# A two-layer encoder on one core: token halves grouped over six tail and eight head k-tiles, and a ring of nine split weight pairs

## The chip, the core and the metric

One core of a Trainium2 chip. The time is the device time of one execution in microseconds (us). The profile is of one execution.

## What is computed

A two-layer encoder for 256 tokens of width 2048, in fp32. Cut to what matters here:

```python
for l in range(2):
    h = rms_norm(x, norm_g[l, 0])
    m = parallel_ab_mixer(h, ...) if l == 0 else chunk_band_attention(h, ...)   # ends in "@ w_out"
    x = x + rms_norm(m, norm_g[l, 1])
    f = (silu(h2 @ w_gate[l]) * (h2 @ w_up[l])) @ w_down[l]   # h2 = rms_norm(x, norm_g[l, 2])
    x = x + rms_norm(f, norm_g[l, 3])
```

rms_norm divides a token's row by its root mean square, so no token of a block's output is finished before that token's whole row of the last product is there.

## The kernel before

The 256 tokens are two halves of 128, t = 0 and 1. Every product is cut into column chunks of 512 and k-tiles of 128 rows. Each weight is read once: SP's queue brings two k-tiles as one `raw` tile of 512 KB (L224, four buffers). ACT casts each k-tile to the fp32r tile `hi` (L230), DVE subtracts to get `lo` (L231). Five such pairs (`wpool`, bufs=5) can be alive. For each k-tile and token half, `mm_chunk` issues three 128x512 matmuls, hi with the activation's hi (L250), lo with its hi (L251), hi with its lo (L252). The two halves alternate k-tile by k-tile, each in its own PSUM tile `mm_...`.

The stages are, in order, w_in with layer 0's mixer, w_oab (4 chunks of 16 k-tiles), w_gu0 (22 chunks of 16), w_dn0 (4 of 44), w_qkv with the attention, w_oc (4 of 16), w_gu1 and w_dn1. w_oab, w_dn0, w_oc and w_dn1 end in `out_norm`, the next stage begins with `pre_norm`.

`out_norm` squares each chunk's rows on ACT (L317) and scales them on DVE. In the last of its four chunks, n = 3, the last four k-tiles have their pairs in a pool E of their own and run all for half 0, then all for half 1. When a half is done: ACT Square (L317) and sqrt (L319), DVE L320 (PSUM times the gain row, into `m`), reciprocal (L321), then four residual operations (L323), one for each column slice of 512; these make the next block's input `m_o_0` to `m_o_3` (`m_fo_...` after an FFN). The very last out_norm sends each piece to HBM.

`pre_norm` takes the four slices one by one. PE transposes 128x128 blocks (L286) into PSUM tiles `pn_...`, each with two k-tiles of both halves. ACT (L268) writes the hi part of a k-tile `sh`, DVE (L269) the lo part `sl`, each 128x256. The norm's scale is applied after the product, so the next stage's first matmuls wait for `sh` and `sl` alone.

The engines run their queues in order. The order is set by the Tile scheduler from priorities: the weight stream is PRI_STREAM (4000) ahead of its place in the program, the norms are PRI_NORM (8000) ahead; waits between engines are semaphores that the framework sets from tile uses.

Of the kernel before, what the change touches and what calls it, by code (L numbers as in the profile page):

```python
# [24 lines left out]
PRI_NORM = 8000  # L25
PRI_FIRST = 100000
# [113 lines left out]
def encoder_body(ctx: ExitStack, tc: tile.TileContext, A):  # L140
# [5 lines left out]
    wpool = ctx.enter_context(tc.tile_pool(name="wpool", bufs=5))  # L146
    S = ctx.enter_context(tc.tile_pool(name="S", bufs=12))
# [116 lines left out]
    def split_evac(ps, sh, sl, kts, g):  # L264
        """ps [P, 2, T] (feature-major) times the feature column g(kt), split into hi and lo."""
        for i, kt in enumerate(kts):
            gc = g(kt)
            last = act.activation(sh[:, kt % 4, :], ps[:, i, :], AF.Copy, scale=gc)  # L268
            dve.scalar_tensor_tensor(sl[:, kt % 4, :], ps[:, i, :], gc, sh[:, kt % 4, :].bitcast(F32),  # L269
                                     op0=ALU.mult, op1=ALU.subtract)  # L270
        return last

    def pre_norm(xt, gname, tag):
        """xt: 4 token-major tiles [P, 2, 512]. Returns split x*g, feature-major, and its row scale."""
        st = []
        evacs.clear()
        for n in range(4):
            sh = S.tile([P, 4, T], F32R, tag="S", name=f"sh_{tag}_{n}")
            sl = S.tile([P, 4, T], F32R, tag="S", name=f"sl_{tag}_{n}")
# [9 lines left out]
            st.append((sh, sl))  # L289
# [10 lines left out]
    def out_norm(ctx2, wname, st, grow, xres, tag, last=False):  # L300
        """x + rms_norm(st @ w) * g; returns 4 token-major tiles."""
        E = ctx2.enter_context(tc.tile_pool(name="E" + tag, bufs=4, reuse_waits="tile"))
# [4 lines left out]
        for n in range(4):  # L307
# [3 lines left out]
            ps = mm_chunk(wname, n, st, tail=E if n == 3 else None)  # L311
# [26 lines left out]
    def ffn(l, xt):  # L338
        st, rs = pre_norm(xt, f"g{l}2", f"f{l}")
        with ExitStack() as mx:  # L340
            hp = mx.enter_context(tc.tile_pool(name=f"ff{l}", bufs=2 * NFF, reuse_waits="tile"))
            hid = []
            for j in range(NFF):
                pg = mm_chunk(f"w_gu{l}", 2 * j, st)
# [19 lines left out]
            return out_norm(mx, f"w_dn{l}", hid, 2 * l + 1, xt, f"fo{l}", last=l == 1)  # L364

# [1 line left out]
    def mixer0(xt):  # L367
# [3 lines left out]
        with ExitStack() as mx:  # L371
# [11 lines left out]
            def proj(n, width=512):  # L383
                """Token-major rows of the in-projection, scaled: [P, 2, 512]."""
# [6 lines left out]
            def tr2(tm, c0s, width=P, name=""):  # L391
                """Two feature tiles, transposed: PSUM [P, 2, T]."""
# [6 lines left out]
            def shift_mix(ps, out, mi, n=P):  # L399
                """out = p + (shift(p) - p) * mu, feature-major [n, T]; mi: column of mu."""  # L400
# [18 lines left out]
            # dt = softplus(p + bias): max(x, 0) + 2 atanh(e / (2 + e)), e = exp(-|x|)  # L419
# [33 lines left out]
            def rwkv_half(hf):  # L453
# [7 lines left out]
                for which in range(3):  # L461
# [20 lines left out]
                    if which == 0:  # L482
                        # decay logs, in-chunk running sums, in-context rates, unit keys
# [56 lines left out]
                        # in-chunk products, masked: rows b|k, columns a|r  # L540
# [11 lines left out]
                        # (I - N)^-1 of the 32-blocks, block (chunk, head) on a partition  # L552
# [15 lines left out]
                # bonus: sum(r k r_k) v  # L568
# [6 lines left out]
                # token-major b|k and v  # L575
# [12 lines left out]
                # S = (I - N)^-1 of the 64-blocks, from the 32-blocks  # L588
# [20 lines left out]
                # chunks in order  # L609
# [61 lines left out]
                # group norm per token and head  # L671
# [42 lines left out]
            def conv_silu(ps, i, ft, out):  # L714
                """Causal 4-tap convolution and SiLU of one feature tile: out [P, T]."""
# [23 lines left out]
            # exp of running sums: to the end of tile 0, from the start of tile 1  # L739
# [66 lines left out]
            for g in range(2):  # L806
# [29 lines left out]
    def mixer1(xt):  # L836
# [3 lines left out]
        with ExitStack() as mx:  # L840
# [3 lines left out]
            for g in range(4):  # L844
# [3 lines left out]
                for which in range(2):  # L848
                    ps2 = mm_chunk("w_qkv", 3 * g + which, st)
# [55 lines left out]
            return out_norm(mx, "w_oc", ost, 2, xt, "o1")  # L905
# [21 lines left out]
```

## Time and profile before

| what | value |
| --- | --- |
| median of 3 runs | 2416.78 us (2416.41 to 2418.41) |
| profiled execution | span 2412.1 us, first to last instruction, 4.7 us less than the median of the runs |
| PE matmul busy | 2372.9 us, 98% |
| DVE, ACT busy | 59%, 53% |
| chain that ended last | PE 94%, DVE 4%, ACT 1% |
| DMA | 178 GB/s mean, 429 MB |
| mean granted TensorE clock | 0.992 |

The time is set by PE. A busy share says little about the places where PE stops; these are found in the list of PE's waits and in the timelines around them. The granted clock is given as a share of full speed: 1.00 is 2.4 GHz and 0.50 is 1.2 GHz.

### The profile page before, as it was taken

To read this page: it belongs to the slowest core of one execution; us is meant where nothing else is said; L and a number is where in the kernel's file an instruction comes from. 1 tells how busy PE (TensorE), PEld (TensorE's weight loads), DVE (VectorE), ACT (ScalarE), POOL (GpSimd) and SP (SyncE) were. 2 spreads that over 40 slices of the span, in tenths; PEclk is the share of its full clock that TensorE was granted. 3 is DMA by queue.
4 is the path that set the end of the run, shared out by engine and by line. 5 is a ranking of instruction groups with operands and counts; after the bars stand their busy time and mean duration, and the time that the engine had idled before them with its cause. 6 is when DMAs were issued, how large, how long until landed. Compare 5 with 4: busy or idle time off the path is not lost.

```text
span 2412.1 us, 31517 instructions
## 1 busy us (share of the span) xinstructions
PE 2372.9 (98%) x11374; PEld 1940.9 (80%) x11374; DVE 1424.3 (59%) x2340; ACT 1267.4 (53%) x2232; POOL 33.2 (1%) x60
## 2 busy tenths in 40 slices
PE   8999999999999999999999999999999999999998
PEld 7777778878888888888877888887888888888887
DVE  5865967665555555555556555556555555555554
ACT  6646545656445445444446555555544544544443
POOL 0000000000000000000000000000000000000000
PEclk9999999999999999999999999999999999999999
DMA  7433424656666666666675555565666666666665
GB/s 229 142 113 112 140 88 132 190 181 189 192 185 191 192 185 191 192 187 196 196 229 153 180 178 160 172 191 172 189 189 189 190 189 191 189 188 193 199 197 158
DMA packets 119358, 429.17 MB, mean 178 GB/s; under 512 B 13409, under 2 KB 13665, under 8 KB 119201
## 3 DMA queue, kind: packets, MB, share of 16 engines
q1 hardware_dynamic: 115424, 415.46, 56.6%
q0 software_dynamic: 2400, 9.18, 1.5%
q10 hardware_dynamic: 1376, 2.52, 0.3%
q8 instruction: 89, 1.46, 0.3%
q14 instruction: 69, 0.56, 0.1%
HBM read 425.01 MB, written 2.10 MB: 177 GB/s over the span
## 4 chain that ended last, share of the span: by engine, by line
PE 94%; DVE 4%; ACT 1%; issue 1%; DMA 1%; SPq 0%; POOL 0%; DVEq 0%; ACTq 0%; POOLq 0%
PE mm_w_gu L250 13%; PE mm_w_gu L252 13%; PE mm_w_gu L251 13%; PE mm_w_dn L251 7%; PE mm_w_dn L252 7%; PE mm_w_dn L250 7%; PE mm_w_qkv L250 4%; PE mm_w_qkv L251 4%; PE mm_w_qkv L252 4%; PE mm_w_in L252 3%; PE mm_w_in L251 3%; PE mm_w_in L250 3%; PE mm_w_oc L252 1%; PE mm_w_oc L251 1%; PE mm_w_oab L251 1%; PE mm_w_oab L252 1%
## 5 line engine op out<-in xcount | busy, mean ns | idle before, releaser
L231 DVE TENSOR_TENSOR lo_w_gu<-raw_w_gu,hi_w_gu 128x512 fp32r<-128x512 f32 x704 | 486.7, 692 | 433.3 <-ACT hi_w_gu L230 432.4
L230 ACT CAST hi_w_gu<-raw_w_gu 128x512 fp32r<-128x512 f32 x704 | 438.3, 623 | 473.4 <-DVE lo_w_gu L231 424.9
L250 PE MATMUL mm_w_gu<-hi_w_gu,sh_f 128*128 128x512 f32 x1408 | 551.3, 392 | 0.7 <-ACT sh_f L268 0.7
L251 PE MATMUL mm_w_gu<-lo_w_gu,sh_f 128*128 128x512 f32 x1408 | 551.3, 392 | 0.0
L252 PE MATMUL mm_w_gu<-hi_w_gu,sl_f 128*128 128x512 f32 x1408 | 549.2, 390 | 0.0
L231 DVE TENSOR_TENSOR lo_w_dn<-raw_w_dn,hi_w_dn 128x512 fp32r<-128x512 f32 x352 | 242.4, 692 | 218.5 <-ACT hi_w_dn L230 218.2
L230 ACT CAST hi_w_dn<-raw_w_dn 128x512 fp32r<-128x512 f32 x352 | 217.2, 621 | 246.5 <-DVE lo_w_dn L231 233.1
L250 PEld LDWEIGHTS mm_w_gu<-hi_w_gu,sh_f 128*128 128x128 f32 x1408 | 265.1, 188 | 55.6 <-ACT sh_f L268 1.2
L252 PEld LDWEIGHTS mm_w_gu<-hi_w_gu,sl_f 128*128 128x128 f32 x1408 | 265.0, 188 | 54.2
L251 PEld LDWEIGHTS mm_w_gu<-lo_w_gu,sh_f 128*128 128x128 f32 x1408 | 265.2, 188 | 53.2
L251 PE MATMUL mm_w_dn<-lo_w_dn,hh 128*128 128x512 f32 x704 | 276.8, 393 | 0.0
L252 PE MATMUL mm_w_dn<-hi_w_dn,hl 128*128 128x512 f32 x704 | 275.3, 391 | 0.0
L250 PE MATMUL mm_w_dn<-hi_w_dn,hh 128*128 128x512 f32 x704 | 274.8, 390 | 0.0
L231 DVE TENSOR_TENSOR lo_w_qkv<-raw_w_qkv,hi_w_qkv 128x512 fp32r<-128x512 f32 x192 | 132.5, 692 | 102.9 <-ACT hi_w_qkv L230 102.6
L230 ACT CAST hi_w_qkv<-raw_w_qkv 128x512 fp32r<-128x512 f32 x192 | 118.9, 621 | 108.6 <-DVE lo_w_qkv L231 65.5
L231 DVE TENSOR_TENSOR lo_w_in<-raw_w_in,hi_w_in 128x512 fp32r<-128x512 f32 x184 | 125.0, 689 | 56.1 <-ACT hi_w_in L230 54.9
L250 PEld LDWEIGHTS mm_w_dn<-hi_w_dn,hh 128*128 128x128 f32 x704 | 132.1, 188 | 30.1
L250 PE MATMUL mm_w_in<-hi_w_in,sh_in 128*128 128x512 f32 (+1 forms) x384 | 154.5, 402 | 1.4 <-ACT hi_w_in L230 1.4
L252 PE MATMUL mm_w_in<-hi_w_in,sl_in 128*128 128x512 f32 (+1 forms) x384 | 155.2, 404 | 0.0
L251 PEld LDWEIGHTS mm_w_dn<-lo_w_dn,hh 128*128 128x128 f32 x704 | 132.3, 188 | 28.4
L251 PE MATMUL mm_w_qkv<-lo_w_qkv,sh_qkv 128*128 128x512 f32 x384 | 155.1, 404 | 0.0
L252 PEld LDWEIGHTS mm_w_dn<-hi_w_dn,hl 128*128 128x128 f32 x704 | 132.2, 188 | 27.8
(335 smaller groups left out, 2837.5 us busy)
## 6 DMA issues: line engine op xcount, KB each, us to landing
raw_w_gu<-in_w_gu SPq DMA_DIRECT2D x352, 512.0 KB, 3.6
raw_w_dn<-in_w_dn SPq DMA_DIRECT2D x176, 512.0 KB, 4.2
raw_w_qkv<-in_w_qkv SPq DMA_DIRECT2D x96, 512.0 KB, 3.6
raw_w_in<-in_w_in SPq DMA_DIRECT2D x92, 512.0 KB, 3.6
raw_w_oab<-in_w_oab SPq DMA_DIRECT2D x32, 512.0 KB, 3.7
raw_w_oc<-in_w_oc SPq DMA_DIRECT2D x32, 512.0 KB, 4.2
bias<-in_bias POOLq DMA_DIRECT2D x4, 768.0 KB, 7.5
x_in<-in_x SPq DMA_DIRECT2D x4, 512.0 KB, 10.3
```

Source lines behind the costliest of these rows:

```text
L230: act.copy(hi, raw[:, h, :])
L231: dve.tensor_tensor(lo, raw[:, h, :], hi.bitcast(F32), op=ALU.subtract)
L250: pe.matmul(o, lhsT=xh, rhs=h_[:, :width], start=k_ == 0, stop=False)
L251: pe.matmul(o, lhsT=xh, rhs=l_[:, :width], start=False, stop=False)
L252: pe.matmul(o, lhsT=xl, rhs=h_[:, :width], start=False, stop=k_ == nk - 1)
```

## The change

Two numbers are added, HEAD = 8 and TAIL = 6. In the last chunk of every out_norm the last six k-tiles run for half 0, then for half 1. In the first chunk of w_gu0, w_qkv and w_gu1 the first eight k-tiles do so. The pool E is gone. From w_oab on (a second pool `wx` is opened when layer 0's mixer pools are closed) the pairs go round a ring of nine, five in `wpool` and four in `wx`; w_in still has five. For slices 0 and 1 of these three pre_norms a PSUM tile `ph_...` holds four k-tiles of one half, with priority PRI_EVAC (9000); its evacuation pieces are 128x128 (L294 on ACT, L295 on DVE, 16 each where eight 128x256 stood). Slices 2 and 3 stay as they were. Comments are removed, which shifts line numbers: L230, L231, L250 to L252, L317 to L323 become L235, L236, L255 to L257, L334 to L340.

```diff
+PRI_EVAC = 9000
+HEAD, TAIL = 8, 6
...
+    ring = [wpool]
+    turn = [0]
...
-            wp = tail if tail is not None and u >= nk // 2 - 2 else wpool
...
                 for h in range(2):
+                    wp = ring[turn[0] % len(ring)]
+                    turn[0] += 1
...
-        skew = 4 if tail is not None else 0
-        for kt, (hi, lo) in enumerate(stream(wname, n, nk, tail)):
+        for kt, (hi, lo) in enumerate(stream(wname, n, nk)):
             held.append((kt, hi, lo))
-            if kt < nk - skew or kt == nk - 1:
+            if head - 1 <= kt < nk - tail or kt == nk - 1:
...
     def pre_norm(xt, gname, tag):
+        split = 0 if tag == "in" else 2
+        for t in range(2):
+            for n in range(split):
+                sh, sl = st[n]
+                with tc.high_priority(offset=PRI_EVAC):
+                    ps = psa.tile([P, 4, P], F32, tag="sa", name=f"ph_{tag}_{n}_{t}")
+                    for i in range(4):
+                        pe.transpose(ps[:, i, :], xt[n][:, t, i * P:(i + 1) * P], ident)
+                    for i in range(4):
+                        gc = col(gname, 4 * n + i)
+                        xh = sh[:, i, t * P:(t + 1) * P]
+                        last = act.activation(xh, ps[:, i, :], AF.Copy, scale=gc)
+                        dve.scalar_tensor_tensor(sl[:, i, t * P:(t + 1) * P], ps[:, i, :], gc, xh.bitcast(F32),
+                                                 op0=ALU.mult, op1=ALU.subtract)
+        for n in range(split, 4):
...
-        E = ctx2.enter_context(tc.tile_pool(name="E" + tag, bufs=4, reuse_waits="tile"))
...
-            ps = mm_chunk(wname, n, st, tail=E if n == 3 else None)
+            ps = mm_chunk(wname, n, st, tail=TAIL if n == 3 else 0)
...
-                pg = mm_chunk(f"w_gu{l}", 2 * j, st)
+                pg = mm_chunk(f"w_gu{l}", 2 * j, st, head=HEAD if j == 0 else 0)
```

**The first boundary, PE.** `mm_w_oab_0` and `mm_w_oab_1` are the two halves of the last w_oab chunk, `mm_w_gu_0_0` and `mm_w_gu_0_1` those of the first w_gu0 chunk; `hi_w_oab_7_1` is the last k-tile. Before:

```order
L251 MATMUL mm_w_oab_1_4642<-lo_w_oab_7_1_4792,ybh_4033 128x512
L286 MATMUL pn_f_0_0_4842<-cc,m_o_0_4254 128x128 x2
L286 MATMUL pn_f_0_1_4851<-cc,m_o_0_4254 128x128 x2
L252 MATMUL mm_w_oab_1_4642<-hi_w_oab_7_1_4791,ybl_4034 128x512
L286 MATMUL pn_f_0_0_4842<-cc,m_o_0_4254 128x128 x2
L286 MATMUL pn_f_0_1_4851<-cc,m_o_0_4254 128x128 x2
L250 MATMUL mm_w_gu_0_0_4946<-hi_w_gu_0_0_0_4950,sh_f_0_4840 128x512
```

After:

```order
L256 MATMUL mm_w_oab_1_4642<-lo_w_oab_7_0_4776,ybh_4033 128x512
L290 MATMUL ph_f_0_0_4847<-cc,m_o_0_4254 128x128 x4
L290 MATMUL ph_f_1_0_4860<-cc,m_o_1_4443 128x128 x4
L257 MATMUL mm_w_oab_1_4642<-hi_w_oab_7_0_4775,ybl_4034 128x512
L255 MATMUL mm_w_oab_1_4642<-hi_w_oab_7_1_4779,ybh_4033 128x512
L256 MATMUL mm_w_oab_1_4642<-lo_w_oab_7_1_4780,ybh_4033 128x512
L257 MATMUL mm_w_oab_1_4642<-hi_w_oab_7_1_4779,ybl_4034 128x512
L255 MATMUL mm_w_gu_0_0_4961<-hi_w_gu_0_0_0_4965,sh_f_0_4839 128x512
```

Half 0's transposes now stand four matmuls ahead of half 1's end and need two residual tiles; half 1's (`ph_f_0_1`, `ph_f_1_1`) stand in the head, 16 matmuls after its first.

**The first boundary, DVE, from half 0's end.** Before:

```order
L231 TENSOR_TENSOR lo_w_gu_0_2_0_4995<-raw_w_gu_0_2_4992,hi_w_gu_0_2_0_4994 128x512
L320 TENSOR_TENSOR m_o_3_4819<-mm_w_oab_0_4641,gb_o_3_4639 128x512
L321 RECIPROCAL rs_o_4073<-rs_o_4073 128x1
L323 SCALAR_TENSOR_TENSOR m_o_0_4254<-m_o_0_4254,rs_o_4073,x_x_0_4060 128x512
L323 SCALAR_TENSOR_TENSOR m_o_1_4443<-m_o_1_4443,rs_o_4073,x_x_1_4062 128x512
L323 SCALAR_TENSOR_TENSOR m_o_2_4630<-m_o_2_4630,rs_o_4073,x_x_2_4064 128x512
L323 SCALAR_TENSOR_TENSOR m_o_3_4819<-m_o_3_4819,rs_o_4073,x_x_3_4066 128x512
L320 TENSOR_TENSOR m_o_3_4819<-mm_w_oab_1_4642,gb_o_3_4639 128x512
```

After:

```order
L337 TENSOR_TENSOR m_o_3_4819<-mm_w_oab_0_4641,gb_o_3_4639 128x512
L338 RECIPROCAL rs_o_4073<-rs_o_4073 128x1
L236 TENSOR_TENSOR lo_w_gu_0_1_1_4980<-raw_w_gu_0_1_4973,hi_w_gu_0_1_1_4979 128x512
L340 SCALAR_TENSOR_TENSOR m_o_0_4254<-m_o_0_4254,rs_o_4073,x_x_0_4063 128x512
L340 SCALAR_TENSOR_TENSOR m_o_1_4443<-m_o_1_4443,rs_o_4073,x_x_1_4065 128x512
L340 SCALAR_TENSOR_TENSOR m_o_2_4630<-m_o_2_4630,rs_o_4073,x_x_2_4067 128x512
L295 SCALAR_TENSOR_TENSOR sl_f_0_4840<-ph_f_0_0_4847,pf,sh_f_0_4839 128x128
L340 SCALAR_TENSOR_TENSOR m_o_3_4819<-m_o_3_4819,rs_o_4073,x_x_3_4069 128x512
L295 SCALAR_TENSOR_TENSOR sl_f_1_4842<-ph_f_1_0_4860,pf,sh_f_1_4841 128x128
L295 SCALAR_TENSOR_TENSOR sl_f_0_4840<-ph_f_0_0_4847,pf,sh_f_0_4839 128x128
L236 TENSOR_TENSOR lo_w_gu_0_3_0_4996<-raw_w_gu_0_3_4993,hi_w_gu_0_3_0_4995 128x512
```

Ahead of half 0's end five `lo` of the next stage were made before (k-tiles 0 to 4) and three are now; the fourth stands between the reciprocal and the first residual, others among the residuals and pieces. On ACT, likewise, the casts of k-tiles 3 to 8 stand behind half 0's sqrt.

**The end of layer 0's mixer, ACT.** `rs_gr` is the last norm's root there, `ybh` the evacuation of the mixer's output. Before:

```order
L260 ACT_TABLE_LOAD
L260 ACTIVATE rs_gr<-rs_gr 128x2
L230 CAST hi_w_in_7_0_3994<-raw_w_in_7_3992 128x512
L230 CAST hi_w_in_7_1_3998<-raw_w_in_7_3992 128x512
L268 ACTIVATE ybh_3816<-yb_3818,pf 128x256
```

After:

```order
L235 CAST hi_w_oab_0_0_4080<-raw_w_oab_0_4078 128x512
L265 ACT_TABLE_LOAD
L265 ACTIVATE rs_gr<-rs_gr 128x2
L235 CAST hi_w_in_7_0_3994<-raw_w_in_7_3992 128x512
L235 CAST hi_w_in_7_1_3998<-raw_w_in_7_3992 128x512
L235 CAST hi_w_oab_1_0_4102<-raw_w_oab_1_4100 128x512
L235 CAST hi_w_oab_0_1_4084<-raw_w_oab_0_4078 128x512
L235 CAST hi_w_oab_2_0_4124<-raw_w_oab_2_4122 128x512
L235 CAST hi_w_oab_1_1_4106<-raw_w_oab_1_4100 128x512
L273 ACTIVATE ybh_3816<-yb_3818,pf 128x256
```

Five casts of w_oab now stand ahead of the first `ybh`, one of them ahead of the sqrt. POOL's and SP's orders are unchanged.

## Rows read from the trace of the kernel before

**Rows 1.** PE's waits: engine, line, waited for, us in total, times, longest.

```profile
PE pn_f L286 <- DVE m_o L323: 5.0, 2, 2.6
...
PE pn_qkv L286 <- DVE m_fo L323: 2.5, 1, 2.5
```

**Rows 2.** Timeline, first boundary, half 0: start, duration, engine, line, operation [idle before].

```profile
521.55 0.39 PE L252 MATMUL mm_w_oab<-hi_w_oab,ybl 128*128 128x512 f32 x1
...
522.70 0.69 DVE L320 TENSOR_TENSOR m_o<-mm_w_oab,gb_o 128x512 f32<-128x512 f32 x1 [2.11 <-ACT junk_o L317]
...
523.50 2.74 DVE L323 SCALAR_TENSOR_TENSOR m_o<-m_o,rs_o,x_x 128x512 f32<-128x512 f32 x4
```

**Rows 3.** Timeline, first boundary, half 1's end and the next stage's start.

```profile
524.78 0.48 PE L252 MATMUL mm_w_oab<-hi_w_oab,ybl 128*128 128x512 f32 x1
525.30 0.60 ACT L317 ACTIVATE junk_o<-mm_w_oab 128x512 bf16<-128x512 f32 x1 [2.30 <-PE mm_w_oab L252]
...
527.75 0.66 PE L286 MATMUL pn_f<-cc,m_o 128*128 128x128 f32 x4 [2.49 <-DVE m_o L323]
...
528.75 0.80 PE L250 MATMUL mm_w_gu<-hi_w_gu,sh_f 128*128 128x512 f32 x1 [0.35 <-ACT sh_f L268]
```

**Rows 4.** Windows after the three boundaries: length, busy us by engine, PEclk, DMA.

```profile
528.00:533.00 5.00, 4.65 (x18) 3.60 (x17) 3.49 (x8) 2.31 (x5) 0.00 (x0) 0.66 0.23 52
1269.00:1273.00 4.00, 4.00 (x14) 3.16 (x13) 2.87 (x6) 1.47 (x3) 0.00 (x0) 0.57 0.12 31
1668.00:1673.00 5.00, 5.00 (x18) 4.00 (x18) 3.38 (x7) 2.15 (x6) 0.00 (x0) 0.66 0.27 54
```

**Rows 5.** PE's timeline after two stops in layer 0's mixer.

```profile
159.02 1.18 PE L599 MATMUL ga<-TG,AA 32*32 32x32 f32 x31 [2.71 <-DVE TG L594]
...
253.91 0.63 PE L396 MATMUL tr<-cc,tm 128*128 128x128 f32 x4 [2.19 <-DVE r L402]
254.29 0.48 PE L250 MATMUL mm_w_in<-hi_w_in,sh_in 128*128 128x512 f32 x1
254.61 0.40 PE L251 MATMUL mm_w_in<-lo_w_in,sh_in 128*128 128x512 f32 x1
254.84 0.39 PE L252 MATMUL mm_w_in<-hi_w_in,sl_in 128*128 128x512 f32 x1
```

**Rows 6.** Windows after these two stops, columns as in rows 4.

```profile
254.00:255.00 1.00, 1.00 (x7) 0.91 (x8) 1.00 (x3) 0.42 (x2) 0.00 (x0) 1.00 0.84 262
...
160.00:165.00 5.00, 5.00 (x77) 4.29 (x75) 0.00 (x0) 1.17 (x3) 0.00 (x0) 0.50 0.35 108
```

**Rows 7.** Instruction groups by form: count, busy us, mean ns, idle before by releaser.

```profile
L231 DVE TENSOR_TENSOR lo_w_gu<-raw_w_gu,hi_w_gu 128x512 fp32r<-128x512 f32 x704 | 486.7, 692 | 433.3 <-ACT hi_w_gu L230 432.4
L230 ACT CAST hi_w_gu<-raw_w_gu 128x512 fp32r<-128x512 f32 x704 | 438.3, 623 | 473.4 <-DVE lo_w_gu L231 424.9 <-PE mm_w_gu L252 40.3 <-DMA raw_w_gu<-in_w_gu 3.8
...
L269 DVE SCALAR_TENSOR_TENSOR sl_f<-pn_f,pf,sh_f 128x256 fp32r<-128x256 f32 x32 | 14.3, 478 | 1.0 <-ACT sh_f L268 0.9
L268 ACT ACTIVATE sh_f<-pn_f,pf 128x256 fp32r<-128x256 f32 x32 | 13.8, 470 | 6.2 <-PE pn_f L286 5.4 <-DVE sl_f L269 0.8
L323 DVE SCALAR_TENSOR_TENSOR m_fo<-m_fo,rs_fo,m_o 128x512 f32<-128x512 f32 x16 | 11.0, 748 | 0.1
...
L902 ACT CAST oh<-ov 128x256 fp32r<-128x256 f32 x16 | 5.6, 375 | 3.8 <-PE ov L901 3.5
```

**Rows 8.** Timeline of the kernel's end.

```profile
2402.49 2.74 DVE L323 SCALAR_TENSOR_TENSOR m_fo<-m_fo,rs_fo,m_o 128x512 f32<-128x512 f32 x4
...
2403.27 0.39 PE L252 MATMUL mm_w_dn<-hi_w_dn,hl 128*128 128x512 f32 x1
...
2404.42 0.29 ACT L319 ACTIVATE rs_fo<-ssq_fo,part_fo 128x1 f32<-128x1 f32 x1
2405.15 0.68 DVE L320 TENSOR_TENSOR m_fo<-mm_w_dn,gb_fo 128x512 f32<-128x512 f32 x1
2405.75 0.15 DVE L321 RECIPROCAL rs_fo<-rs_fo 128x1 f32<-128x1 f32 x1
```

More of the change, by code (lines that the diff above doesn't have):

```diff
@@ L211, in encoder_body, with stream @@
     dve.tensor_scalar(hcv, pf[:, _PF["conv_w"]:_PF["conv_w"] + 60], 0.5, None, op0=ALU.mult)
-    def stream(wname, n, nk, tail=None):
+    def stream(wname, n, nk):
         src = A[wname]
         for u in range(nk // 2):
-            wp = tail if tail is not None and u >= nk // 2 - 2 else wpool
             with tc.high_priority(offset=PRI_STREAM):
@@ L233, in stream, with mm_chunk @@
             yield from pair
-    def mm_chunk(wname, n, st, width=512, tail=None):
+    def mm_chunk(wname, n, st, width=512, head=0, tail=0):
         nk = 4 * len(st)
@@ L273, in pre_norm @@
     def pre_norm(xt, gname, tag):
-        st = []
+        st = [(S.tile([P, 4, T], F32R, tag="S", name=f"sh_{tag}_{n}"),
+               S.tile([P, 4, T], F32R, tag="S", name=f"sl_{tag}_{n}")) for n in range(4)]
         evacs.clear()
-        for n in range(4):
-            sh = S.tile([P, 4, T], F32R, tag="S", name=f"sh_{tag}_{n}")
-            sl = S.tile([P, 4, T], F32R, tag="S", name=f"sl_{tag}_{n}")
+        split = 0 if tag == "in" else 2
[13 more added lines that the diff above has]
+        for n in range(split, 4):
+            sh, sl = st[n]
             with tc.high_priority(offset=PRI_NORM):
@@ L288, in pre_norm @@
                     evacs.append(last)
-            st.append((sh, sl))
         ssq = sm.tile([P, 2, 4], F32, tag="ssq", name=f"ssq_{tag}")
@@ L298, in pre_norm, with out_norm @@
         return st, rsqrt_mean(ssum, D, EPS, "pre", [P, 2])
-    def out_norm(ctx2, wname, st, grow, xres, tag, last=False):
-        E = ctx2.enter_context(tc.tile_pool(name="E" + tag, bufs=4, reuse_waits="tile"))
+    def out_norm(wname, st, grow, xres, tag, last=False):
         ssq = sm.tile([P, 2, 4], F32, tag="ssq", name=f"ssq_{tag}")
@@ L363, in ffn @@
                 hid.append((sh, sl))
-            return out_norm(mx, f"w_dn{l}", hid, 2 * l + 1, xt, f"fo{l}", last=l == 1)
+            return out_norm(f"w_dn{l}", hid, 2 * l + 1, xt, f"fo{l}", last=l == 1)
     def mixer0(xt):
@@ L830, in mixer0 @@
                 yst.append((sh, sl))
+        wx = ctx.enter_context(tc.tile_pool(name="wx", bufs=4, reuse_waits="tile"))
+        ring[:] = [wpool, wx, wpool, wx, wpool, wx, wpool, wx, wpool]
         with ExitStack() as mx:
             xres = load_x(mx.enter_context(tc.tile_pool(name="X0", bufs=4, reuse_waits="tile")), "x0")
-            return out_norm(mx, "w_oab", yst, 0, xres, "o0")
+            return out_norm("w_oab", yst, 0, xres, "o0")
     def mixer1(xt):
@@ L848, in mixer1 @@
                 for which in range(2):
-                    ps2 = mm_chunk("w_qkv", 3 * g + which, st)
+                    ps2 = mm_chunk("w_qkv", 3 * g + which, st, head=HEAD if g + which == 0 else 0)
                     tm = B.tile([P, 2, 512], F32, tag="tm", name=f"qk{g}{which}")
@@ L904, in mixer1 @@
                 ost.append((sh, sl))
-            return out_norm(mx, "w_oc", ost, 2, xt, "o1")
+            return out_norm("w_oc", ost, 2, xt, "o1")
     x1 = mixer0(x_in)
```

## The prediction

> **What bounds the kernel now.** The table above says that PE is busy for 98% of the span and that the chain which ended last is PE for 94% of its length. Matmuls of 128x512 start 0.23 us apart when nothing stops them [rows 5]. The change adds and removes none of them, so it can move the time only where PE stops, or where it runs at the lower clock. I therefore read PE's waits first. The transposes at the head of a stage wait for the residual tiles `m_o` and `m_fo`: 5.0 us in two waits and 2.5 us in one [rows 1], that is about 2.5 us at each of the three boundaries w_oab to w_gu0, w_dn0 to w_qkv and w_oc to w_gu1.
>
> The timeline of the first boundary shows the chain behind one wait. Half 0 ends with the matmul at 521.55, its scaling L320 starts 1.15 us later, its four residuals 1.95 us later [rows 2]. Half 1 ends 12 matmuls after half 0, with the matmul at 524.78. Its own chain (L317, sqrt, L320, L321, L323) only delivers `m_o_0` of half 1 at 527.75, so PE stands for 2.49 us. After four transposes it stands again, for 0.35 us, until ACT has evacuated the first tile [rows 3]. Last, I read the clock. In the 5, 4 and 5 us after these stops the mean granted clock is 0.66, 0.57 and 0.66 [rows 4], so (1 - 0.66) x 5, (1 - 0.57) x 4 and again 0.34 x 5 = 1.7 us of full-rate work is lost each time.
>
> One boundary thus costs 2.5 + 0.35 of waiting, 1.7 of half clock, and about 0.1 for each of two restarts (the first two matmuls after a stop start 0.32 apart where later ones are 0.23 apart [rows 5]): **4.75 us**, 14.2 us for three.
>
> **The change at a boundary.** With six k-tiles grouped instead of four, half 0 ends two k-tiles, 6 x 0.23 = 1.4 us, earlier and its chain starts 1.4 us earlier. With eight k-tiles grouped in the first chunk, the new order of PE has 16 matmuls (3.7 us) of half 0 ahead of half 1's transposes. That covers half 1's chain of 3.0 us (524.78 to 527.75), so the long stop goes. What is late next is the work that makes the head's operands. I walk it in the clock of [rows 2, 3].
>
> Half 0's last matmul starts at 521.55 - 1.4 = 520.2, L337 at 521.3, the reciprocal ends near 522.1. In the new order of DVE the `lo` of k-tile 3 stands ahead of the first residual. Its cast takes a ring slot that half 1's first tail k-tile gives back, and ACT is with Square and sqrt until about 521.6 (sqrt ends 1.44 us after the half's last matmul has started, as from 2403.27 to 2404.71 [rows 8]). Cast 0.62 and `lo` 0.69 [rows 7] bring DVE to 522.9; with residuals 0.685 apart (2.74 for four [rows 2]) `m_o_0` is there at 523.6 and `m_o_1` at 524.3. PE has then done 14 of its 18 half-1 matmuls (520.4 + 14 x 0.23 = 523.6), transposes `m_o_0` (0.38 [rows 5]) and waits some 0.35 for `m_o_1`. The last four matmuls end at 525.7, and the head begins.
>
> Its evacuation pieces are 128x128, which no row has. From 128x256 and 128x512 of a like kind [rows 7] DVE's is 478 - (748 - 478)/2 = 343 ns and ACT's 470 - (623 - 375)/2 = 346 ns: my estimate is 0.35 each, the other end is the full 0.47. Four pieces lie in one PSUM tile, where ACT and DVE take turns, so a k-tile is ready every 0.35 + 0.35 + two hand-offs = 0.8 us, more when a cast, Square (0.60 [rows 3]) or a residual stands between, while PE eats a k-tile of one half in 0.69. k-tiles 0 and 1 are in time; I count 0.4 for k-tile 2 and 0.55 for k-tile 3, 0.35 for the second pair of transposes (`m_o_0` of half 1 stands behind L337, the reciprocal, a `lo` and three pieces), and 0.75 for the first k-tiles of half 1 and k-tile 4. With the 0.35 above that is **2.4 us** of waiting. About eight stops at 0 to 0.1 for a restart: 0.4. The boundary then costs 2.8 instead of 4.75, **1.95 less, 5.85 for three**, if the clock stays up.
>
> The ends of this term: in the stretch DVE has 8 residuals (5.5), L337 (0.7), 16 pieces (5.5) and some five `lo` (3.5), together 15.2 us, against PE's 66 matmuls (15.2) and 16 transposes (1.5), 16.7 us. DVE fits, but with little room. If all overlaps, only 0.35 and 0.65 of it are left (1.0). If it queues badly, or the pieces cost 0.47 each, 16 x 0.12 = 1.9 more on DVE, of which 1.5 shows (4.2).
>
> Why does this not vanish as the ring grows? Nine pairs hold six tail pairs and three of the head; before, four tail pairs lay in pool E and five of the head were cast in advance. Five casts of the head's eight therefore fall into the boundary where three did.
>
> **The clock.** A stop of 2.19 us before 253.91 was followed by a clock of 1.00, and a stop of 2.71 before 159.02 by 0.50 from 160 to 165 [rows 5, 6]. The walk leaves no stop over 0.6, with full matmuls between them, and the first three of a head together (0.35 + 0.4 + 0.55) are shorter than the one that kept 1.00. I take the 1.7 as won in full.
>
> The Trainium skill, page "TensorE: Matmul & The Clock Gate", section "A second HAM failure mode: psum-queue depth-cycling", speaks against this: it tells of a kernel whose PE idles briefly but often between groups of matmuls and whose clock swings between the two levels. No row of before has such a run of short stops, so it stands as a rival below; by it the 1.7 would be paid again.
>
> **The other parts.** *End of the kernel.* The last out_norm gets the six-tile tail without a head. In before L320 of half 1 starts only at 2405.15, behind half 0's four residuals (2402.49 + 2.74), though sqrt ended at 2404.71 [rows 8]. With half 0 1.4 us earlier the residuals end at 2403.9, L320 by 2404.5, and the reciprocal waits for sqrt: it starts near 2404.75 instead of 2405.75. **1.0 less**; between 0.7 (a hand-off more) and 1.2. *Ring.* From w_oab on four more casts stand ahead of mixer0's last work on ACT: one ahead of the sqrt that the first `yb` transposes wait for (0.62 [rows 7]), twice at most, the rest ahead of evacuations that PE needs only in w_oab's later k-tiles. 0 to 1.2; with what deeper casting displaces in the attention stage (0 to 0.8) I take **+0.8**. *FFN stages.* Casts run up to nine k-tiles ahead; the list behind [rows 1] has no wait of PE for a cast of these stages, and ACT idles as long as it casts [rows 7], so 0. *DMA, POOL and SP* keep their order and `raw` its four buffers: 0.
>
> **Sum.** -5.85 - 1.0 + 0.8 = -6.05 us. The profiled execution has a span of 2412.1, the median of the runs is 4.7 us longer; I take what lies around the span as unchanged, so from 2416.78 the forecast is **2410.7 us**. A measurement can tell about 0.2% (4.8 us, so below 2411.95) from no change.
>
> **The rivals.**
> *B, the clock falls once per head.* For it: eight stops and 16 transposes in some 9 us, nothing like which before shows. Against it: the 2.19 us stop. Price 1.7 x 3 = 5.1, so 2415.8, within 0.2%.
> *D, DVE and ACT become the bound.* For it: 15.2 us of DVE work in 16.7, and the strict turns in a PSUM tile. Against it: ACT's 16 pieces (5.5), two Squares with accumulator and sqrt (2.2) and five casts (3.1) are 10.8 us of the 16.7. Price 4.2 - 2.4 = 1.8 of which some 1.1 shows at each boundary, so +3.3: 2414.0, within 0.2%.
> *C, slower.* The clock drops at the first stops and stays low until the stops end: some 8.5 us of head and then 3.4 as in [rows 4], 12 us at half clock, as it stayed at 0.50 from 160 to 165 and beyond under a stream of small work [rows 6]. It costs 6.0 less the 1.6 of waits that slower matmuls hide, 4.4 x 3 = 13.2: 2423.9. It is slower from 11 us in all, 3.7 per boundary. Against it: the matmuls in the head are full ones.
> *N, nothing gained.* The transposes put among the last half-1 matmuls wait longer than 0.35 and move the old stop ahead: every 0.7 us (one residual more ahead of `m_o_1`) costs 2.1; 2412.8 with one, counted under D.
>
> **How the numbers follow.** The forecast's case gets 0.66; its own spread, waits of 1.6 to 3.4 us per boundary (2.4 less to 3.0 more in three) and the bounds of the small terms, is 2407.5 to 2414, of which 0.52 lies below 2411.95 and 0.14 above. B gets 0.12, D with N 0.15 (0.02 of it below the line), C 0.07. Faster 0.54, same 0.39, slower 0.07. The range reaches up to B with a little over it and down to the forecast's lower end: 2407.0 to 2416.2; C lies outside.
>
> **What will show it.** PE's waits for `m_o` of 2.5 us are gone and 5 to 9 waits of 0.1 to 0.6 each stand at a boundary, on `sh_f`, `sl_f` and `ph_f`, 2.4 us in all (1.0: overlap better than walked; 4: D). The granted clock stays 1.00 in the 15 us after each (0.50 in any: B or C). The last reciprocal starts 1.0 us nearer to the last matmul (2405.75 - 2403.27 = 2.5 now [rows 8], 1.5 then). Wrong would be new PE waits for casts in the FFN stages, or stops where the ring opens above 1.2 us.

## The result: slower, with the long stops gone

The changed kernel takes 2437.11 us (median of 4 runs, 2435.0 to 2438.2), the kernel before on the same chip 2417.28. The ratio is 1.008, 95% interval 1.0065 to 1.0094. I forecast 2410.7, faster, with a range up to 2416.2: wrong in sign and outside the range. One execution of the kernel before (2960.93 us) and one of a variant (13552.62 us) lie far outside all others and are left out of the medians below.

The page of the changed kernel, first its span and engines:

```profile
span 2433.2 us, 31534 instructions
...
PE 2400.9 (99%) x11374; PEld 1937.6 (80%) x11374; DVE 1425.6 (59%) x2364; ACT 1267.9 (52%) x2256; POOL 33.2 (1%) x60
```

The span grew by 21.1 us, and PE's busy time by 28.0 (from 2372.9) for the same 11374 matmuls. So PE does not wait more; its matmuls take longer. The list of PE's waits (us in total, times, longest) confirms the first half. Its only rows on the boundaries and the ring are:

```profile
PE yb L845 <- DVE xs L837: 0.8, 1, 0.8
PE mm_w_gu L255 <- ACT sh_f L294: 0.5, 2, 0.3
...
PE mm_w_qkv L255 <- ACT sh_qkv L294: 0.2, 1, 0.2
```

The waits of 5.0 and 2.5 us for the residual tiles [rows 1] are gone. The windows over the three boundaries (length, busy us of PE, PEld, DVE, ACT, POOL, then granted clock, DMA share, GB/s) show that the half clock of [rows 4] is gone too:

```profile
528.00:543.00 15.00, 14.63 (x69) 9.89 (x68) 14.37 (x34) 9.94 (x28) 0.54 (x1) 1.00 0.39 116
...
1276.00:1286.00 10.00, 9.66 (x44) 6.10 (x42) 9.86 (x24) 6.53 (x20) 0.54 (x1) 1.00 0.29 79
1676.00:1686.00 10.00, 9.65 (x45) 6.25 (x43) 9.91 (x24) 6.58 (x19) 0.54 (x1) 1.00 0.29 79
```

Now a stretch in which PE waits for nothing, 400 us in the middle of w_gu0, instructions on its PSUM tiles alone (length, then PE, PEld, DVE, ACT, clock). The kernel before:

```profile
600.00:1000.00 400.00, 396.03 (x1727) 322.66 (x1726) 12.63 (x18) 12.10 (x18) 1.00 0.63 189
```

The changed kernel:

```profile
600.00:1000.00 400.00, 396.30 (x1697) 316.57 (x1696) 12.63 (x18) 12.35 (x18) 1.00 0.62 186
```

At the same clock, 30 matmuls fewer fit: 231.6 us per thousand before, 235.7 now (the transposes between them included). The length of each stage, from its first to its last matmul start in the two traces, gives the account:

| stage | before | after | change, us |
| --- | --- | --- | --- |
| ahead of w_oab | 436.1 | 439.6 | +3.5 |
| w_oab | 88.6 | 90.8 | +2.2 |
| w_gu0, w_gu1 | 492.8, 492.9 | 501.8, 501.7 | +17.7 |
| w_dn0, w_dn1 | 242.9, 242.4 | 245.6, 244.5 | +4.9 |
| w_qkv with the attention | 303.7 | 307.2 | +3.4 |
| w_oc | 91.0 | 92.5 | +1.5 |
| from one stage to the next, w_oab on | 12.6 | 1.4 | -11.3 |
| last matmul start to the end | 8.78 | 8.08 | -0.7 |

The 29.6 us in the stages from w_oab on are the loss. Some 4 of them come with the new order, the short stops and the transposes that moved into the stages, and stand against the 11 us saved between the stages (in two kernels compared below, which differ by the change but not in the spacing of their matmuls, it is 3.7). The other 26 are spread over all stages. Of the 3.5 us ahead of w_oab 0.7 is a later start and 0.8 the new wait for `xs`; the rest goes with more half clock in layer 0's mixer, where the order is unchanged. One window there, of the changed kernel:

```profile
250.00:262.00 12.00, 9.81 (x50) 6.98 (x49) 10.72 (x20) 5.04 (x10) 1.97 (x4) 0.86 0.55 174
```

The same window of the changed kernel with 64 unused bytes (below), after the same stop of 2.19 us:

```profile
250.00:262.00 12.00, 9.81 (x64) 7.33 (x63) 12.00 (x23) 5.05 (x10) 1.97 (x4) 1.00 0.57 175
```

**Which matmuls are slow.** PE's timeline of the changed kernel in the same stage, two k-tiles (start, duration, line, operation):

```profile
800.70 0.39 PE L255 MATMUL mm_w_gu<-hi_w_gu,sh_f 128*128 128x512 f32 x1
800.94 0.39 PE L256 MATMUL mm_w_gu<-lo_w_gu,sh_f 128*128 128x512 f32 x1
801.17 0.39 PE L257 MATMUL mm_w_gu<-hi_w_gu,sl_f 128*128 128x512 f32 x1
...
802.10 0.39 PE L255 MATMUL mm_w_gu<-hi_w_gu,sh_f 128*128 128x512 f32 x1
802.33 0.40 PE L256 MATMUL mm_w_gu<-lo_w_gu,sh_f 128*128 128x512 f32 x1
...
803.48 0.39 PE L255 MATMUL mm_w_gu<-hi_w_gu,sh_f 128*128 128x512 f32 x1
```

The first k-tile (800.70 to 802.10, six matmuls) has its pair in `wx`: 1.40 us, 233 ns a matmul. The second (802.10 to 803.48) has it in `wpool`: 1.38, 230 ns. Taken over all of w_gu0, the six matmuls of a k-tile start 233.3 ns apart in each of the four `wx` slots, 230 on average in the `wpool` slots that follow a `wx` slot, and 226.7 in the one that follows a `wpool` slot. In the kernel before all are 226.8. Nothing in the order, the clock or the waits distinguishes them. What differs is where the tiles lie.

The compiler puts `wpool` at 38080 bytes in each partition, the norm tiles `sh`, `sl` from 58560 on, `wx` at 112768. All starts of weight and norm tiles in the kernel before leave 192 when divided by 256; `wx` leaves 128. That is one lead, and that `wx` is far from the norm tiles is another.

### The profile page after: what moved, and what is told of

It reads as the page before. It is cut to its first block, busy times and chain, and to the rows that moved or that the text cites. A ratio compares the mean times of both kernels' runs of the same rounds, so it can differ in the third digit from the quotient of the medians.

```text
span 2433.2 us, 31534 instructions
## 1 busy us (share of the span) xinstructions
PE 2400.9 (99%) x11374; PEld 1937.6 (80%) x11374; DVE 1425.6 (59%) x2364; ACT 1267.9 (52%) x2256; POOL 33.2 (1%) x60
## 4 chain that ended last, share of the span: by engine, by line
PE 93%; DVE 3%; ACT 1%; DMA 1%; issue 1%; SPq 0%; POOL 0%; DVEq 0%; ACTq 0%; POOLq 0%
PE mm_w_gu L256 13%; PE mm_w_gu L255 13%; PE mm_w_gu L257 13%; PE mm_w_dn L255 7%; PE mm_w_dn L257 7%; PE mm_w_dn L256 7%; PE mm_w_qkv L255 4%; PE mm_w_qkv L256 4%; PE mm_w_qkv L257 4%; PE mm_w_in L257 3%; PE mm_w_in L256 2%; PE mm_w_in L255 2%; PE mm_w_oc L255 1%; PE mm_w_oab L256 1%; PE mm_w_oc L257 1%; PE mm_w_oab L255 1%
## 5 line engine op out<-in xcount | busy, mean ns | idle before, releaser
L236 DVE TENSOR_TENSOR lo_w_gu<-raw_w_gu,hi_w_gu 128x512 fp32r<-128x512 f32 x704 | 486.3, 692 | 434.2 <-ACT hi_w_gu L235 432.8
L235 ACT CAST hi_w_gu<-raw_w_gu 128x512 fp32r<-128x512 f32 x704 | 436.3, 621 | 474.8 <-PE mm_w_gu L257 420.4
L255 PE MATMUL mm_w_gu<-hi_w_gu,sh_f 128*128 128x512 f32 x1408 | 555.4, 394 | 0.6 <-ACT sh_f L294 0.5
L257 PE MATMUL mm_w_gu<-hi_w_gu,sl_f 128*128 128x512 f32 x1408 | 551.6, 392 | 0.0
L236 DVE TENSOR_TENSOR lo_w_dn<-raw_w_dn,hi_w_dn 128x512 fp32r<-128x512 f32 x352 | 243.1, 692 | 230.1 <-ACT hi_w_dn L235 230.1
L235 ACT CAST hi_w_dn<-raw_w_dn 128x512 fp32r<-128x512 f32 x352 | 217.8, 620 | 258.5 <-PE mm_w_dn L257 213.7
L255 PEld LDWEIGHTS mm_w_gu<-hi_w_gu,sh_f 128*128 128x128 f32 x1408 | 263.9, 187 | 65.4 <-ACT sh_f L294 3.4
L257 PEld LDWEIGHTS mm_w_gu<-hi_w_gu,sl_f 128*128 128x128 f32 x1408 | 264.2, 188 | 60.8 <-DVE sl_f L295 1.2
L255 PE MATMUL mm_w_dn<-hi_w_dn,hh 128*128 128x512 f32 x704 | 278.8, 396 | 0.0
L257 PE MATMUL mm_w_dn<-hi_w_dn,hl 128*128 128x512 f32 x704 | 277.0, 394 | 0.0
L236 DVE TENSOR_TENSOR lo_w_qkv<-raw_w_qkv,hi_w_qkv 128x512 fp32r<-128x512 f32 x192 | 132.3, 691 | 101.1 <-ACT hi_w_qkv L235 101.1
L235 ACT CAST hi_w_qkv<-raw_w_qkv 128x512 fp32r<-128x512 f32 x192 | 118.6, 619 | 105.2 <-PE mm_w_qkv L257 94.2
L236 DVE TENSOR_TENSOR lo_w_in<-raw_w_in,hi_w_in 128x512 fp32r<-128x512 f32 x184 | 124.8, 688 | 56.3 <-ACT hi_w_in L235 54.9
L257 PEld LDWEIGHTS mm_w_dn<-hi_w_dn,hl 128*128 128x128 f32 x704 | 132.3, 188 | 31.6
L255 PE MATMUL mm_w_in<-hi_w_in,sh_in 128*128 128x512 f32 (+1 forms) x384 | 154.6, 403 | 1.4 <-ACT hi_w_in L235 1.4
L257 PE MATMUL mm_w_in<-hi_w_in,sl_in 128*128 128x512 f32 (+1 forms) x384 | 155.4, 405 | 0.0
L255 PEld LDWEIGHTS mm_w_dn<-hi_w_dn,hh 128*128 128x128 f32 x704 | 132.0, 188 | 28.7
```

## The experiments

Times are medians. The runs were made in three groups, each on a chip of its own, where the kernel before has 2414.29 us (64 bytes in either kernel, the grouped ring, the ring alone), 2416.49 us (weight pairs moved, all operands moved, 192 and 32 bytes) and 2415.88 us (320 bytes and all of the last experiment). "Spacing" is the mean start-to-start of successive 128x512 matmuls in a trace, without gaps over 245 ns.

### The address: 64 bytes ahead of `wx`

```diff
+        pad = ctx.enter_context(tc.tile_pool(name="pad", bufs=1))
+        pad.tile([P, 16], F32, tag="pad", name="pad")
         wx = ctx.enter_context(tc.tile_pool(name="wx", bufs=4, reuse_waits="tile"))
```

> The changed kernel with one unused tile of 64 bytes per partition opened ahead of the pool wx, so that the four wx pairs and all pools opened later start 64 bytes further on; the order of work is the same. In the changed kernel the 128x512 matmuls start 233 ns apart where their weight pair lies in wx (start address a multiple of 128) and the activation tile starts 64 bytes past a multiple of 128; they start 227 ns apart where both lie 64 past. Theory A (the start addresses' residue modulo 128 of the two operands sets the spacing): with the pad all operands lie 64 past, all spacings go back to 227, w_gu by 9 us each, and w_dn and w_oc, which were at 229 in both kernels, fall to 227 too: about 2437 - 28.7 - 5.2 = 2403 us. Theory R (the part of the partition: operands above 110 KB against operands below it): 2437, unchanged. Theory M (PE reads one pool while ACT and DVE write the other): 2437, unchanged.

Measured: 2403.58 us, ratio to before 0.9955 (0.9942 to 0.9967). The spacing is 226.7 to 226.9 in w_oab, w_gu, w_dn and w_oc, whichever pools the two operands lie in (227.9 in w_qkv, against 227.6 before). The expectation was wrong in one point: w_dn and w_oc were not at 229 in both kernels, but at 228.9 before and 230.9 after; why is told under the ring's order. The same stretch of w_gu0:

```profile
600.00:1000.00 400.00, 396.01 (x1727) 322.54 (x1726) 12.63 (x18) 12.38 (x18) 1.00 0.62 189
```

64 unused bytes per partition turn 20 us slower into 11 us faster. Distance (R) and two pools as such (M) are out, since both are unchanged.

### The same 64 bytes in the kernel before

The pad stands behind the pools `wpool`, `S`, `sm`, so the FFN's hidden tiles and the attention's outputs move, and pool E with them.

```diff
     psa = ctx.enter_context(tc.tile_pool(name="psa", bufs=2, space=PSUM))
+    pad = ctx.enter_context(tc.tile_pool(name="pad", bufs=1))
+    pad.tile([P, 16], F32, tag="pad", name="pad")
```

> The kernel before with an unused tile of 64 bytes per partition ahead of the pools that are opened stage by stage (the FFN's hidden tiles, the attention's outputs); weight pairs and norm tiles stay where they are. Theory A: the w_dn and w_oc matmuls go from 229 to 227 ns, 2500 of them by 2.1 ns: 2417 - 5.2 = 2412 us. Theories R and M: unchanged, 2417.

Measured: 2409.19 us, ratio 0.9981 (0.9972 to 0.999), 5.1 us less than the kernel before on that chip. w_dn0 between 1050 and 1250 us, before:

```profile
1050.00:1250.00 200.00, 200.00 (x875) 164.13 (x874) 4.15 (x6) 4.11 (x12) 1.00 0.67 203
```

and with the pad:

```profile
1050.00:1250.00 200.00, 200.00 (x884) 165.62 (x883) 4.15 (x6) 4.11 (x12) 1.00 0.67 205
```

Nine more matmuls in 200 us. So the kernel before carried the same loss in a place that no wait shows.

### None of the change, only the weight pairs moved

```diff
+    pad = ctx.enter_context(tc.tile_pool(name="pad", bufs=1))
+    pad.tile([P, 16], F32, tag="pad", name="pad")
     wpool = ctx.enter_context(tc.tile_pool(name="wpool", bufs=5))
+    pad2 = ctx.enter_context(tc.tile_pool(name="pad2", bufs=1))
+    pad2.tile([P, 16], F32, tag="pad2", name="pad2")
```

> The kernel before, none of the change in it, with 64 unused bytes ahead of wpool and 64 more behind it: only the weight pairs (and raw) move, to a multiple of 128; the norm tiles stay 64 past one, the FFN and attention tiles stay on one. Theory A (spacing by whether the two operands have the same residue): w_in, w_oab, w_gu and w_qkv go from 227 to 233 ns, 6500 matmuls by 6.4 ns, while w_dn and w_oc go from 229 to 227: about 2415 + 41 - 5 = 2451 us. If it needed the second pool or the longer ring: 2415.

Measured: 2446.49 us, ratio 1.0127 (1.0098 to 1.0157), 30 us slower. The spacing is 233.3 in w_in, w_oab, w_gu and w_qkv, 226.7 in w_dn and w_oc. 35 was expected; that counted all of w_in's matmuls, though this stage also has waits (its mean with gaps of up to 600 ns is 238 ns before) which may hide a part. The stretch of w_gu0:

```profile
600.00:1000.00 400.00, 396.31 (x1682) 313.13 (x1681) 12.65 (x18) 12.36 (x18) 1.00 0.62 185
```

No second pool, no longer ring, and a larger loss than the change's own.

### All operands moved together

The first of the two pads alone.

> The kernel before with 64 unused bytes ahead of wpool alone: every operand of the products moves by 64, so each pair of operands keeps its difference (w_gu both on a multiple of 128, w_dn 0 and 64). If the difference counts: all spacings and the time as before, 2415. If an operand must itself lie 64 past a multiple of 128: w_in, w_oab, w_gu and w_qkv slow down, over 2430.

Measured: 2416.93 us, ratio 1.0009 (0.9998 to 1.002), spacing 226.9 in w_gu and 228.9 in w_dn as before. It is the difference between the starts that counts, not a start.

### The modulus: 192, 32 and 320 bytes

The pad ahead of `wx` with `[P, 48]`, `[P, 8]` and `[P, 80]`.

> The changed kernel with a pad of 192 bytes ahead of wx in place of 64: wx has the norm tiles' residue modulo 128 but not modulo 256 or 512. Theory A modulo 128: all spacings 227 and the time of the 64-byte pad, about 2403. If the modulus is 256 or more: 233 in w_gu, about 2432.

> The changed kernel with a pad of 32 bytes ahead of wx: residue 32, half-way between. No theory says more than its name here: A modulo 128 gives spacings above 227 for pairs in wx (between 229 and 233), A modulo 32 would give 227; the time lies between 2403 and 2437.

> The changed kernel with a pad of 320 bytes ahead of wx: start addresses in wx and in wpool or the norm tiles then differ by a multiple of 256 and not of 512 (with 64 bytes they differ by a multiple of 512, with 192 by 128 more than one of 256). If the modulus that counts is 256: all spacings 227 and a span near 2400 as with 64 bytes. If it is 512: above 229 in w_gu, span over 2425.

Measured, one run each: 2432.35, 2437.96 and 2405.48 us. 192 bytes give the same remainder by 128 as 64 bytes do and are slow, so "modulo 128" in the theory's name was wrong. 320 bytes are as good as 64: the spacing is 226.7 to 226.9 in the same four stages, so of these candidates the modulus is 256. The stretch of w_gu0, with 192 bytes:

```profile
600.00:1000.00 400.00, 396.28 (x1704) 318.36 (x1703) 12.63 (x18) 12.34 (x18) 1.00 0.62 187
```

and with 320:

```profile
600.00:1000.00 400.00, 396.02 (x1728) 322.61 (x1727) 12.64 (x18) 12.38 (x18) 1.00 0.63 189
```

All kernels together, by the start of the stationary tile less the start of the moving tile, modulo 256 (the stationary tile is the activation's, the moving tile the weight's; the addresses are the compiler's, no view of a profile shows them):

| difference | spacing, ns | where |
| --- | --- | --- |
| 0 | 226.7 to 226.9 | w_gu before, all stages with 64 or 320 bytes |
| 32 | 233.6 | `wx` pairs in w_gu, 32 bytes |
| 64 | 233.3 to 233.4 | `wx` pairs in w_gu after, all of w_gu with `wpool` moved, pool E in w_oab before |
| 128 | 232.0, 233.3 | 192 bytes: `wx` pairs in w_gu, `wpool` pairs behind a `wpool` pair in w_dn |
| 192 | 228.9 | w_dn, w_oc before |
| 224 | 233.5 | `wpool` pairs behind a `wpool` pair in w_dn, 32 bytes |

### Reading one pool while writing the other

```diff
-        ring[:] = [wpool, wx, wpool, wx, wpool, wx, wpool, wx, wpool]
+        ring[:] = [wpool] * 5 + [wx] * 4
```

> The changed kernel with the ring's slots in the order five of wpool, then four of wx, in place of alternating ones; addresses are unchanged. While PE reads one slot, ACT and DVE refill the slot before it, so now PE reads and they write the same pool in seven slots of nine, where it was one of nine. Theory M (crossing pools is what costs): nearly all of the 23 us in w_oab, w_gu and w_qkv goes, about 2416. Theories A and R: pairs in wx stay at 233, and only the smaller loss of the wpool slots beside them falls from four slots to one: about 2431.

Measured: 2425.39 us, ratio 1.0043 (1.0029 to 1.0057): 11 us above the kernel before, against 20 for the alternating ring. Theory A's 2431 was 14 above the 2417 that it was reckoned from, M's 2416 was 1 below; 11 speaks for A. By slot in w_gu: the `wx` slots stay at 233.3, four `wpool` slots are at 227, and only the first, which runs while `wx`'s last slot is refilled, is at 230 (its six spacings are 226, 235, 229, 232, 230 and 227). So there is a second effect: where PE's own operands agree, it is still slowed while ACT and DVE write a tile with another remainder.

This second effect is not small in the changed kernel. In w_gu it makes about a third of the loss (four slots of nine at 230, beside four at 233.3), and no other cause is seen for the loss in w_dn and w_oc. There the `wx` pairs have the remainder of the stationary tiles and the `wpool` pairs keep the difference of the kernel before, so by the operands alone the spacing should have fallen below 228.9; it rose to 230.9. The same stretch of w_dn0 as above, of the changed kernel, with 868 matmuls where the kernel before had 875:

```profile
1050.00:1250.00 200.00, 200.00 (x868) 162.66 (x867) 4.15 (x6) 4.11 (x12) 1.00 0.66 202
```

Its `wx` slots are at 231.5, though their operands agree, while a `wpool` slot is refilled; in the grouped ring the four `wx` slots of w_dn, of which only the first runs while a `wpool` slot is refilled, are at 231.6, 230.2, 227.0 and 226.8 (the second's 230.2 is not explained). That the writing does it is inferred from these slots; a run that changes the writes alone was not made.

### The ring alone

```diff
-HEAD, TAIL = 8, 6
+HEAD, TAIL = 1, 4
...
-        split = 0 if tag == "in" else 2
+        split = 0
```

> The changed kernel with HEAD = 1, TAIL = 4 and the norms' evacuation as it was before; the ring of nine in two pools stays. Theory that the ring's placement costs (A, R or M alike): the spacing of 233 stays and the gain at the boundaries goes, 2417 + 29 = 2446 us, with clock falling at the boundaries again. Rival H (the grouped halves or the casts further ahead slow the stages): without the groups near 2417.

Measured: 2446.62 us, ratio 1.0131 (1.0116 to 1.0147). The spacing is that of the changed kernel, 231.1 in w_gu. So rival H is out: without the groups the kernel is no faster, and the casts run as far ahead with the 64 bytes, where nothing is lost. The ring in its place costs 32 us over the kernel before; tail and head gave back about 12 of them.

### What tail, head and half tiles are worth with addresses in step

All with the 64 bytes ahead of `wx`. Tail of four:

```diff
-HEAD, TAIL = 8, 6
+HEAD, TAIL = 8, 4
```

> The 64-byte pad with TAIL = 4 in place of 6, HEAD = 8. Five of the head's pairs are cast ahead instead of three, but half 0's chain starts 1.4 us later. Theory that late casts hold the head: the boundary's cost beyond its matmuls (6.3 us with 6) falls to about 5.5, time about 2 us below the 64-byte pad. Theory that half 0's chain holds it: the transposes ahead of half 1's last matmuls wait 1 us more, 7.3, and the time is 3 us above; at the kernel's end 0.7 us come back on top.

Tail without head, with `split = 0` as above:

```diff
-HEAD, TAIL = 8, 6
+HEAD, TAIL = 1, 6
```

> The 64-byte pad with TAIL = 6, but HEAD = 1 and the evacuation in pieces for both halves as before: only tail and ring are left. The stop of 2.5 us for half 1's residuals and the fall of the clock come back at the three boundaries, the cost beyond the matmuls rises from 6.3 to about 9, the kernel's end stays 0.7 shorter: about 8 us above the 64-byte pad.

Tail and head without the tiles for one half (`split = 0` alone):

> The 64-byte pad with TAIL = 6 and HEAD = 8, but the evacuation in pieces of both halves (no tiles for one half). If the tiles for one half carry the gain: the first matmul of half 0 again needs half 1's transposes, the 2.5 us stop is back, span about 2407. If the order of the matmuls alone did it: span near 2400.

The boundary's cost is the time from the first matmul of the last out_norm chunk to the first of the next stage's second chunk, less 192 matmuls (360 at w_dn0) of 226.7 ns. It contains 32 transposes in every kernel. The end is from the last matmul's start to the end of the span. Both are of one profile each. The times of the first two rows and of the last three are from two chips, on which the kernel before differs by 1.6 us.

| kernel | three boundaries, us | end, us | time, us |
| --- | --- | --- | --- |
| before, 64 bytes | 8.8, 8.7, 8.9 | 8.8 | 2409.19 |
| changed, 64 bytes | 6.3, 6.3, 6.3 | 8.0 | 2403.58 |
| tail of four | 6.6, 6.6, 6.6 | 8.8 | 2406.06 |
| tail alone | 10.0, 9.1, 9.3 | 8.0 | 2411.39 |
| no half tiles | 9.0, 8.8, 9.1 | 8.1 | 2413.57 (one run) |

PE's waits without half tiles show the old stop back, longer than in [rows 1]:

```profile
PE pn_f L305 <- DVE m_o L340: 5.9, 2, 3.0
PE pn_qkv L305 <- DVE m_fo L340: 2.9, 1, 2.9
```

The head together with its half tiles carries the 2.5 us of each boundary; its order of matmuls without them gives nothing. Half tiles without that order were not run. Of the time without half tiles 4.5 us lie ahead of w_oab, where its one profile is longer. A tail of four, with five pairs cast ahead instead of three, costs 0.3 more, not the 0.8 less or 1.0 more of the two theories. That fits casts and half 0's chain weighing about the same; it does not show it.

## Why the prediction was wrong, step by step

**The step that failed** stands in its first paragraph: the change adds and removes no matmul, "so it can move the time only where PE stops, or where it runs at the lower clock", and with it "FFN stages ... so 0". That treats the 0.23 us between matmuls as a constant of the chip. It is a property of where the two operands lie and, by the ring's slots, of what is written meanwhile, and a new pool moves both. The term that I put at 0 measured some 26 us (stages +29.6, less the 3.7 of the new order).

**The trace of before showed it.** The tail's four k-tiles of pool E ran in a stretch that I read for [rows 2]. The kernel before, a little ahead of those rows:

```profile
518.98 0.39 PE L250 MATMUL mm_w_oab<-hi_w_oab,ybh 128*128 128x512 f32 x1
...
520.15 0.39 PE L252 MATMUL mm_w_oab<-hi_w_oab,ybl 128*128 128x512 f32 x1
...
521.32 0.39 PE L251 MATMUL mm_w_oab<-lo_w_oab,ybh 128*128 128x512 f32 x1
```

Ten matmuls take 2.34 us, 234 ns each. The kernel before in w_gu0:

```profile
803.48 0.39 PE L252 MATMUL mm_w_gu<-hi_w_gu,sl_f 128*128 128x512 f32 x1
...
805.07 0.39 PE L250 MATMUL mm_w_gu<-hi_w_gu,sh_f 128*128 128x512 f32 x1
```

Seven take 1.59, 227 ns each. Rounded to 0.23 the two look alike; times all 9312 such matmuls the difference is 60 us. A bound of 0 to 3% on the spacing of pairs in a new pool (four slots of nine, some 8300 matmuls: up to 25 us) would have brought the range near the true time and put its sign into the rivals. Instead none of my rivals had a steady loss.

**The boundaries.** Right, and rather too cautious. With the addresses in step a boundary costs 2.5 us less (8.8 to 6.3) where I had 1.95. The walk of the head holds in the main in the changed kernel's timeline (first boundary):

```profile
526.24 0.69 DVE L337 TENSOR_TENSOR m_o<-mm_w_oab,gb_o 128x512 f32<-128x512 f32 x1 [3.54 <-ACT junk_o L334]
526.44 2.48 ACT L235 CAST hi_w_gu<-raw_w_gu 128x512 fp32r<-128x512 f32 x4
...
527.69 2.07 DVE L340 SCALAR_TENSOR_TENSOR m_o<-m_o,rs_o,x_x 128x512 f32<-128x512 f32 x3
...
528.58 1.29 PE L290 MATMUL ph_f<-cc,m_o 128*128 128x128 f32 x8
...
533.42 0.50 PE L255 MATMUL mm_w_gu<-hi_w_gu,sh_f 128*128 128x512 f32 x1 [0.26 <-ACT sh_f L294]
```

The residuals start 1.45 us after L337 (1.6 in the walk), behind a cast and a `lo`. k-tile 3's first matmul starts at 533.42, 0.65 us after the one ahead of it. The pieces of 128x128 measure 371 ns on ACT and 344 on DVE, where I had 346 and 343. Most of the short waits stand at the weight loads, not at the matmuls, so the list of waits shows fewer than I announced. The view of the tile `mm_w_gu` counts both (two boundaries: until, us, times):

```profile
its engine sat idle before it (us, times) until:
  ACT sh_f L294: 3.9, 10
  DVE sl_f L295: 1.2, 4
  DVE lo_w_gu L236: 0.3, 1
```

That is at most 2.7 us a boundary, since a stop can be counted at a load and at its matmul; the walk had 1.7 for these. The loads of the transposes wait 0.9 a boundary for `m_o` by the same view of `ph_f` (1.8 us in two), where the walk had 0.7. So the waits were not put too high; why the gain is larger than forecast is not shown.

**The clock.** Right: 1.00 through all three boundaries, so rivals B and C fell. The Trainium skill's oscillation (page "TensorE: Matmul & The Clock Gate", section "A second HAM failure mode: psum-queue depth-cycling") did not appear under these stops. But one of the rows that I leaned on, 1.00 after the stop of 2.19 us, was a chance: the windows from 250 to 262 above show 0.86 and 1.00 after the same stop. That stops like the heads', 0.6 us and less, leave the clock at 1.00 is shown by the heads alone.

**The end of the kernel.** 0.7 us (8.78 to 8.08), where I had 1.0:

```profile
2425.12 0.40 PE L257 MATMUL mm_w_dn<-hi_w_dn,hl 128*128 128x512 f32 x1
...
2426.28 0.69 DVE L337 TENSOR_TENSOR m_fo<-mm_w_dn,gb_fo 128x512 f32<-128x512 f32 x1 [0.65 <-ACT junk_fo L334]
...
2426.88 0.15 DVE L338 RECIPROCAL rs_fo<-rs_fo 128x1 f32<-128x1 f32 x1
```

L337 waits for Square, which reads the same PSUM tile, as L320 already did in [rows 2]. The reciprocal starts 1.76 us after the last matmul, against 2.48 in [rows 8] and 1.5 in the forecast.

**The ring's opening.** One new wait for `xs` of 0.8 us; I had +0.8 with the attention's part, which did not show: the +3.4 us of w_qkv are its longer spacing (227.6 to 231.2 ns).

**The sum without the failed term.** From the padded kernel before to the padded changed kernel: 2409.19 to 2403.58, -5.6 us in the medians and -8.0 in the two profiled spans (2407.4 and 2399.4), against the -6.05 of the forecast. The change as it was meant is worth about that, and with 64 bytes ahead of `wx` it beats both kernels.

## What to carry to other kernels

Before pricing a change that opens or moves a pool, take the start-to-start time of the hottest instruction to the nanosecond, separately for each pool that its operands lie in; a spread of 3% there outweighs any stop at a stage's edge. If busy time grows at an unchanged count and clock, look at start addresses before looking at order or waits. Here it helped to keep all matmul operands of a stage, and what is written meanwhile, at the same remainder by 256 bytes, and one small unused tile was enough to do it.

## What the runs showed of the hardware

128x512 fp32r matmuls with a fresh stationary tile each start 226.7 ns apart if the two operands' start addresses agree modulo 256 bytes and tiles with the same remainder are written meanwhile, and 228.9 to 233.6 ns apart at the five other differences that were run. In the nine kernels that were compared for it the spacing went with the difference of the operands' remainders, but for the slots whose operands agree while another remainder is written (230 in w_gu, 231.5 in w_dn of the changed kernel). The two even spacings, 226.7 and 233.3, differ by some 6.7 ns, 16 periods at 2.4 GHz; single spacings in mixed slots lie mostly between 224 and 238. What is shared inside the chip was not shown.

The Trainium skill (page "SBUF — State Buffer", section "Who interferes with whom") gives TensorE two independent read ports, one for the moving operand and one for the weight load. No run here shows what the ports are, but the measured 233 against 227 ns, with nothing changed but 64 bytes, speaks against independence in effect; the measurement decides. The same section of the Trainium skill says that "PE and ACT never wait on anyone"; the 230 ns of slots whose operands agree speak against that too, as far as the inference from the writes holds. The Trainium skill's page "TensorE: Matmul & The Clock Gate" (section "Back-to-back issue gap") gives the spacing by the free size and does not speak of addresses; in these runs it ranges from 226.7 to 233.6 ns at one free size.

The fall of the clock after a stop of 2.2 to 2.5 us is not certain. For the shorter one the two windows from 250 to 262 above differ. In the kernel with all operands moved the third boundary had the same stop, but kept 1.00 (first and third boundary):

```profile
528.00:535.00 7.00, 4.16 (x14) 3.00 (x13) 5.83 (x11) 2.78 (x7) 0.54 (x1) 0.79 0.15 37
...
1666.00:1673.00 7.00, 4.10 (x21) 2.86 (x20) 6.92 (x13) 2.75 (x7) 0.54 (x1) 1.00 0.15 37
```
